# A two-layer encoder on one core: mean squares by f32 matmuls at both ends, and a new table of places

## The chip, the cores and the metric

The kernel runs on one core of a Trainium2 chip. The metric is the device time of one execution in microseconds (us), the median of several runs. The engines are TensorE (PE, with its weight loads as PEld), VectorE (DVE), ScalarE (ACT), GpSimd (POOL) and SyncE (SP, which here only starts transfers). Each works through its own list of instructions in order; an instruction waits until what it reads is there and what it overwrites is no longer needed.

## The reference

Two layers over 1024 tokens of width 1024, in float32. Each normalises, mixes tokens, and adds the result behind a gate; the first layer has two groups of attention heads side by side, the second an attention in a window of 128 tokens to either side with a sink. Cut to what matters here:

```python
def rms_norm(x, g):
    xf = x.astype(jnp.float32)
    y = xf * lax.rsqrt(jnp.mean(xf * xf, axis=-1, keepdims=True) + EPS)
    return (y * g.astype(jnp.float32)).astype(x.dtype)
...
    c_act = jax.nn.silu(c)
    for layer in range(DEPTH):
        mod = c_act @ ada_w[layer] + ada_b[layer]
        shift, scale, gate = jnp.split(mod, 3, axis=-1)
        h = rms_norm(x, norm_w[layer]) * (1.0 + scale[:, None, :]) + shift[:, None, :]
        ...  # y = even_mixer(h, ...) or odd_mixer(h, ...)
        x = x + gate[:, None, :] * y
    return rms_norm(x, final_norm)
```

The change concerns the mean of squares of the first norm (first half of the tokens) and of the last norm (last block), and the order of all work. The values computed stay the same.

## The kernel before

The activations lie transposed, features in the 128 partitions and tokens along the row: xT00 to xT03 hold the first 512 tokens, two chunks of 128 features each (128x1024), xT10 to xT13 the other 512. Every product of float32 matrices is made from three matmuls in a rounded format (fp32r): each operand is split in a high part (h, a cast) and a low part (l, operand minus high part), and high×high, low×high and high×low add up in PSUM.

The program in order: the input is loaded, its mean squares give r = (mean + eps)^-0.5 per token, h = x·r·scale + shift is built chunk by chunk (hT00h/l, ...), where scale and shift (mods) come from DVE's operations on blocks of the modulation weights (ada...). Products with the first layer's combined weights follow: w1x (416 columns, c1), w3x (512, c3) and w2 (256, c2), x the pair of feature chunks. Then the first group's attention (q, k; hl, V), the second group's (latent: khh, kll, Qa/Pa and Qb/Pb with VA/VB), the output projection in seven block products by sums and differences (a, b, s, t with numbers; o and og are the attention outputs, xr the residual rows), the second layer (T6, T7 and hT1x are its normalised inputs, wf its weights, p its windowed scores), its output projection, and the last norm.

A mean over features is a sum over partitions and chunks. At the start, ACT squares each chunk, DVE adds the squares chunk by chunk into two sums (sq0 and the last chunk's sq07), PE transposes them, and DVE reduces the transposed rows (ss), scales and adds eps; POOL raises to the power -0.5 (r, with mhalf as exponent), PE transposes r's columns, widened by broadcast, back to rows, and DVE multiplies x by them. The end has the same steps for the last block of 256 tokens, xr110 to xr113: rstd_rows and finish, called from layer1_after. xr112 is multiplied on POOL with a copy (rbz) made by ACT, the others on DVE.

Order and placing: nothing is issued where it is written. The class Recorder takes every operation down (so each instruction bears one line, L825, where emit calls it). run plans them against the engines with a duration for each from cost, and knows that DVE and POOL share a way into SBUF (held). placed then takes the steps named in PLACES out of the planned order and puts each directly behind the step it names; the pairs are (step, step ahead of it). banks_in hands out the eight banks of PSUM in the order that results; the result is fixed as the program. Transposes of the identity (warm, WARM = how many at three places of the start) compute nothing that is used; they keep PE at work.

## Time and profile before

| what | value |
|---|---|
| median of 3 runs | 1132.55 us (1132.31 to 1133.89) |
| profiled execution | 1132.69 us |
| its span | 1130.9 us |
| granted TensorE clock, mean | 0.99 |
| PE, DVE, ACT, POOL busy | 1097.5, 991.7, 749.0, 681.9 us |
| bytes moved by DMA | 183.71 MB, 162 GB/s in the mean |

The span is what the trace shows of the execution, and lies 1.8 us below its time. The page divides it into 40 slices of 28.3 us. A busy PE need not be at its peak: below full granted clock the same instructions take longer and still count as busy. Since all work bears line 825, it is told apart by the tiles it names: out<-in.

### The profile page before, as it was taken

To read this page: it belongs to the slowest core of one execution; us is meant where nothing else is said; L and a number is where in the kernel's file an instruction comes from. 1 tells how busy PE (TensorE), PEld (TensorE's weight loads), DVE (VectorE), ACT (ScalarE), POOL (GpSimd) and SP (SyncE) were. 2 spreads that over 40 slices of the span, in tenths; PEclk is the share of its full clock that TensorE was granted. 3 is DMA by queue.
4 is the path that set the end of the run, shared out by engine and by line. 5 is a ranking of instruction groups with operands and counts; after the bars stand their busy time and mean duration, and the time that the engine had idled before them with its cause. 6 is when DMAs were issued, how large, how long until landed. Compare 5 with 4: busy or idle time off the path is not lost.

```text
span 1130.9 us, 17581 instructions
## 1 busy us (share of the span) xinstructions
PE 1097.5 (97%) x5914; PEld 935.5 (83%) x5914; DVE 991.7 (88%) x1645; ACT 749.0 (66%) x1462; POOL 681.9 (60%) x666
## 2 busy tenths in 40 slices
PE   7999989999999999999999999999999999999996
PEld 6898977888877878888888878888888888887885
DVE  6978798898999989998999999998878777778997
ACT  4653444777776787887797832667677776766723
POOL 1136776989986644345546445757666775976523
PEclk8999999999999999999999999999999999999998
DMA  9978862574656196769878376301111211249403
GB/s 365 364 186 286 278 232 71 140 181 140 159 157 183 22 279 194 195 172 250 211 177 319 89 213 245 143 1 36 40 57 39 94 57 57 94 145 333 147 1 149
DMA packets 60026, 183.71 MB, mean 162 GB/s; under 512 B 7200, under 2 KB 9632, under 8 KB 58912
## 3 DMA queue, kind: packets, MB, share of 16 engines
q1 hardware_dynamic: 54464, 159.00, 40.8%
q0 software_dynamic: 4608, 22.02, 10.7%
q10 hardware_dynamic: 864, 1.57, 0.4%
q8 instruction: 46, 0.75, 0.3%
q14 instruction: 44, 0.36, 0.1%
HBM read 147.31 MB, written 70.91 MB: 193 GB/s over the span
## 4 chain that ended last, share of the span: by engine, by line
PE 81%; DVE 11%; DMA 4%; issue 2%; ACT 1%; SPq 0%; POOL 0%; POOLq 0%; DVEq 0%; ACTq 0%
PE psum L825 81%; DMA ada<-in_ada_t 2%; DVE nm L825 1%; DVE hla L825 1%; DMA w31s<-in_w_c 1%; DVE xr L825 1%; DMA w33s<-in_w_c 1%; DVE hf L825 1%; DMA relt<-in_tabs_d 1%; DVE t40l L825 0%; DVE w2l L825 0%; DVE psum L825 0%; DVE krt L825 0%; DVE s31l L825 0%; DVE T7l L825 0%
## 5 line engine op out<-in xcount | busy, mean ns | idle before, releaser
L825 DVE TENSOR_REDUCE nm<-psum 128x1 f32<-128x1024 f32 x128 | 155.5, 1218 | 16.1 <-PE psum L825 13.9
L825 POOL TENSOR_SCALAR Pb<-Pb,rs 128x1024 f32<-128x1024 f32 x64 | 75.3, 1187 | 64.6 <-DVE rs L825 57.7
L825 POOL TENSOR_SCALAR p<-p,dn 128x384 f32<-128x384 f32 (+1 forms) x128 | 70.5, 571 | 36.2 <-DVE dn L825 36.1
L825 POOL TENSOR_SCALAR Pa<-Pa,rs 128x1024 f32<-128x1024 f32 x64 | 76.4, 1222 | 25.5 <-DVE rs L825 20.9
L825 ACT ACTIVATE Pa<-psum,nm 128x1024 f32<-128x1024 f32 x64 | 71.8, 1122 | 27.7 <-DVE nm L825 18.5
L825 DVE TENSOR_TENSOR hla<-psum,hla 128x512 fp32r<-128x512 f32 x128 | 82.8, 682 | 4.8 <-ACT hla L825 4.2
L825 DVE CUSTOM_DVE_ANT_0 p<-psum,relt,sinkn 128x384 f32<-128x384 f32 (+1 forms) x128 | 70.6, 578 | 17.2 <-PE psum L825 16.5
L825 DVE TENSOR_TENSOR hlb<-psum,hlb 128x512 fp32r<-128x512 f32 x128 | 81.9, 680 | 3.2 <-ACT hlb L825 2.9
L825 PE MATMUL psum<-hla,VA 128*128 128x512 f32 x256 | 81.6, 410 | 2.9 <-DVE hla L825 2.8
L825 ACT ACTIVATE Pb<-psum,nm 128x1024 f32<-128x1024 f32 x64 | 71.9, 1124 | 17.1 <-DVE nm L825 12.2
L825 ACT ACTIVATE p<-p,nm 128x385 f32<-128x385 f32 (+1 forms) x128 | 74.8, 591 | 9.4 <-POOL p L825 4.9
L825 ACT CAST hla<-psum 128x512 fp32r<-128x512 f32 x128 | 70.0, 597 | 15.7 <-PE psum L825 13.6
L825 PE MATMUL psum<-k,q 128*128 128x512 f32 x256 | 80.3, 396 | 0.1
L825 PE MATMUL psum<-hlb,VB 128*128 128x512 f32 x256 | 79.6, 411 | 0.1
L825 PE MATMUL psum<-ident,Pa 128*128 128x128 f32 x512 | 74.5, 275 | 2.3 <-DVE cqT L825 2.2
L825 PEld LDWEIGHTS psum<-ident,Pa 128*128 128x128 f32 x512 | 62.0, 142 | 13.4 <-issue 2.8
L825 ACT CAST hlb<-psum 128x512 fp32r<-128x512 f32 x128 | 68.8, 605 | 4.4 <-PE psum L825 3.6
L825 ACT COPY ot<-psum 64x512 f32<-64x512 f32 x64 | 37.4, 584 | 50.1 <-PE psum L825 49.3
L825 ACT CAST hl<-psum 128x512 fp32r<-128x512 f32 x88 | 48.4, 590 | 33.0 <-PE psum L825 26.1
L825 DVE TENSOR_TENSOR hl<-psum,hl 128x512 fp32r<-128x512 f32 x88 | 57.7, 685 | 13.7 <-ACT hl L825 12.7
L825 PE MATMUL psum<-ident,Pb 128*128 128x128 f32 x512 | 69.0, 272 | 0.0
L825 PEld LDWEIGHTS psum<-ident,Pb 128*128 128x128 f32 x512 | 60.2, 141 | 8.0 <-ACT Pb L825 0.4
(1146 smaller groups left out, 3721.9 us busy)
## 6 DMA issues: line engine op xcount, KB each, us to landing
ada<-in_ada_t SPq DMA_DIRECT2D x32, 512.0 KB, 9.7
fs<-in_w_f POOLq DMA_DIRECT2D x12, 768.0 KB, 9.1
adag<-in_ada_t SPq DMA_DIRECT2D x16, 512.0 KB, 5.1
ws<-in_w_out POOLq DMA_DIRECT2D x16, 512.0 KB, 6.8
S<-ws SPq DMA_DIRECT2D x16, 512.0 KB, 5.3
A<-in_w_out SPq DMA_DIRECT2D x12, 512.0 KB, 6.7
o<-spill SPq DMA_DIRECT2D x12, 512.0 KB, 6.0
fs<-in_w_f SPq DMA_DIRECT2D x6, 768.0 KB, 8.5
```

Source lines behind the costliest of these rows:

```text
L825: fn(*[real(v) for v in a], **{k: real(v) for k, v in kw.items()})
```

## The change

Seven things change.

1. PLACES is another table, found by a search that the code doesn't contain; and a string BANKS gives each PSUM tile the bank to start from. cost gives a matmul that is not fp32r at least 222 ns.
2. The mean squares at the start: PE sums over partitions itself. share is a column of 128 values 1/1024; a matmul with a 128x128 block of squares as the weights and share as the moving operand adds the means of 128 tokens in one column of PSUM. 28 such f32 matmuls (8 for sq00, 8 for sq01, 4 for sq02, whose two chunks POOL adds first, 8 for sq03) replace six additions on DVE, eight transposes and two reductions. The second half of xT02's and xT03's squares moves from ACT to DVE; xT00 and xT01 are squared in one instruction each.
3. The tail: the last block's sum and the last square go through four such matmuls, with no reduction.
4. WARM goes from 32, 14, 8 to 18, 8, 6, tied by dependences: 18 ahead of the cb transposes, 8 behind the last mean-square matmul and ahead of r's transposes, 6 behind those and ahead of the first products. 54 identity transposes become 32.
5. The first chunk's multiplication by r and the high part of h are made in two halves of 256 tokens.
6. SP's first six transfers are the same in both (xT00, cols, xT01, xT02, xT03, ada000); of those behind, w10s goes ahead of w33s and w11s goes up by four places.
7. Elsewhere steps move by a few places on each engine, all with the same work.

PE at the start, before, with the products of the first chunk below (w10h, w10l: weights; ident alone: warming):

```order
L825 MATMUL psum_72<-ident_73 128x128 x31
L825 MATMUL psum_72<-ident_73,cs_82 128x128 x4
L825 MATMUL psum_72<-ident_73 128x128
L825 MATMUL psum_72<-ident_73,cs_82 128x128 x4
L825 MATMUL psum_72<-ident_73 128x128 x2
L825 MATMUL psum_72<-ident_73,sq07_130 128x128 x4
L825 MATMUL psum_72<-ident_73,sq0_124 128x128 x4
L825 MATMUL psum_72<-ident_73 128x128 x4
L825 MATMUL psum_72<-ident_73,r_133 128x128 x4
L825 MATMUL psum_72<-ident_73 128x128 x12
L825 MATMUL psum_72<-w10h0_137,hT00h0_89 128x416
```

and in the change:

```order
L899 MATMUL psum_72<-ident_73 128x128 x18
L899 MATMUL psum_72<-ident_73,cs_84 128x128 x8
L899 MATMUL psum_72<-share_80,sq00_126 128x1 x8
L899 MATMUL psum_72<-share_80,sq01_127 128x1 x8
L899 MATMUL psum_72<-share_80,sq02_128 128x1 x4
L899 MATMUL psum_72<-share_80,sq03_129 128x1 x8
L899 MATMUL psum_72<-ident_73 128x128 x8
L899 MATMUL psum_72<-ident_73,r_131 128x128 x4
L899 MATMUL psum_72<-ident_73 128x128 x6
L899 MATMUL psum_72<-w10h0_135,hT00h0_91 128x416
```

The transposes of sq07 and sq0 have become matmuls with share, in four groups that follow the four transfers; no warming transpose stands among the products any more.

On DVE at the start, w10l now stands ahead of ss, ada001 between ss and the multiplications of xT00, and w30l and ada011 between those and hT00l; before, ss came ahead of ada001, and w10l and w30l behind the multiplication of xT00.

DVE in the second group's attention, where block 5's hla are made (hla, low parts; nm, row maxima; krt, the rotated shared key), before:

```order
L825 TENSOR_TENSOR hla504_675<-psum_72,hla504_675 128x512
L825 TENSOR_TENSOR hla505_676<-psum_72,hla505_676 128x512
L825 TENSOR_TENSOR krt_723<-krt_723 128x256
L825 TENSOR_TENSOR hla506_677<-psum_72,hla506_677 128x512
L825 TENSOR_TENSOR hla507_678<-psum_72,hla507_678 128x512
L825 TENSOR_REDUCE nm_705<-psum_72 128x1
L825 TENSOR_TENSOR og('0', 2)_633<-psum_72,ot50_695 64x512
```

and in the change:

```order
L899 TENSOR_TENSOR hla504_673<-psum_72,hla504_673 128x512
L899 TENSOR_TENSOR hla505_674<-psum_72,hla505_674 128x512
L899 TENSOR_TENSOR hla506_675<-psum_72,hla506_675 128x512
L899 TENSOR_TENSOR hla507_676<-psum_72,hla507_676 128x512
L899 TENSOR_REDUCE nm_703<-psum_72 128x1
L899 TENSOR_TENSOR krt_721<-krt_721 128x256
L899 TENSOR_TENSOR og('0', 2)_631<-psum_72,ot50_693 64x512
```

The last krt has gone from between hla505 and hla506 to behind nm.

DVE in the first layer's output projection (xr, the residual's rows; psum<-psum,sa, sums of block products; t40l, a low part for a later product), before:

```order
L825 TENSOR_TENSOR psum_72<-psum_72,sa00_1342 128x512
L825 SCALAR_TENSOR_TENSOR xr010_1322<-psum_72,ngcol_88,xr010_1322 128x512
L825 TENSOR_TENSOR t40l1_1389<-o003_1345,t40h1_1388 128x512
L825 TENSOR_TENSOR psum_72<-psum_72,sa00_1342 128x512
L825 SCALAR_TENSOR_TENSOR xr010_1322<-psum_72,ngcol_88,xr010_1322 128x512
```

and in the change:

```order
L899 TENSOR_TENSOR psum_72<-psum_72,sa00_1340 128x512
L899 SCALAR_TENSOR_TENSOR xr010_1320<-psum_72,ngcol_90,xr010_1320 128x512
L899 TENSOR_TENSOR psum_72<-psum_72,sa00_1340 128x512
L899 SCALAR_TENSOR_TENSOR xr010_1320<-psum_72,ngcol_90,xr010_1320 128x512
L899 TENSOR_TENSOR t40l1_1387<-o003_1343,t40h1_1386 128x512
L899 TENSOR_TENSOR t40l1_1387<-og('0', 7)_1254,t40h1_1386 128x512
```

t40l, which stood between the first and the second pair of psum and xr010, now stands behind both.

The diff, with the table cut to its first lines:

```diff
@@ -52,7 +52,7 @@
 K2_POOL = 1
 MOD_WAY = (("dve",), ("psum",))
 E_START = (4, 4)
-WARM = (32, 14, 8)
+WARM = (18, 8, 6)
 SQ_ENG = ("dve", "pool", "pool")
 OLO_POOL = (((0, 0), (1, 0), (2, 0)), ((0, 0), (1, 0), (2, 0)))
 C2_EARLY = 4
@@ -78,265 +78,337 @@
...
-    (48, -1), (324, 105), (110, 324), (2, 1), (78, 17), (79, 78), (80, 79), (81, 80), (82, 81), (83, 82), (84, 83),
...
+    (34, -1), (99, 93), (314, 99), (31, 33), (102, 22), (136, 102), (38, 136), (171, 38), (25, 51), (30, 25),
...
+BANKS = (
...
 )
@@ -512,7 +584,7 @@
             lhs = [r for r in regs if r[0] is kw.get("lhsT")][0]
             c = n / 2.4 + 12.5
             if "float32r" not in str(lhs[6].dtype):
-                c = 4 * n / 2.4 + 12.5
+                c = max(4 * n / 2.4 + 12.5, 222)
             return c, 0
         if eng == "SP":
@@ -783,6 +855,8 @@
     def banks_in(self, seq):

         left, seen, before = {}, set(), dict(self.bank_of)
+        if BANKS:
+            before = {x: int(b) for x, b in zip(self.banks, "".join(BANKS))}
         for o in self.ops:
             for x in o.tiles:
@@ -862,6 +936,8 @@
     make_identity(tc.nc, ident)
     mhalf = const.tile([P, 16], F32, name="mhalf")
     tc.nc.vector.memset(mhalf, -0.5)
+    share = const.tile([P, 1], F32, name="share")
+    tc.nc.vector.memset(share, 1.0 / D)
@@ -953,6 +1029,16 @@
     nc.sync.dma_start(out=cols, in_=cols_d)
     mods = const.tile([P, 32], F32, name="mods")

+
+    def warm(n, behind_):
+        pt = PT(f"warm{n}")
+        for _ in range(n):
+            t_ = nc.tensor.transpose(out=pt[:, 0:P], in_=ident, identity=ident)
+            t_.deps.update(o.i for o in behind_)
+            behind_ = [t_]
+        return behind_
+
+    warmed = warm(WARM[0], [])

     cs = SM("cs")
     nc.scalar.activation(cs[:, 0:8], cols[:, C_C:C_C + 8], AF.Tanh, scale=0.5)
@@ -962,8 +1048,9 @@
     for j in range(2):
         pt = PT(f"cb{j}")
         for k in range(4):
-            nc.tensor.transpose(out=pt[:, k * P:(k + 1) * P], identity=ident,
-                                in_=cs[:, 8 + 4 * j + k:9 + 4 * j + k].broadcast_to([P, P]))
+            t_ = nc.tensor.transpose(out=pt[:, k * P:(k + 1) * P], identity=ident,
+                                     in_=cs[:, 8 + 4 * j + k:9 + 4 * j + k].broadcast_to([P, P]))
+            t_.deps.update(o.i for o in warmed)
         nc.vector.tensor_copy(cb[:, j * 512:(j + 1) * 512], pt)
     nwh = const.tile([P, 16], F32, name="nwh")
     nc.gpsimd.tensor_scalar(nwh, cols[:, C_NW:C_NW + 16], 0.5, 0.0, op0=ALU.mult, op1=ALU.add)
@@ -976,17 +1063,6 @@
     ngcol = const.tile([P, 16], F32, name="ngcol")


-    def warm(n, mark):
-        pt = PT(f"warm{mark.i}")
-        with rec.at(shift=5000), issue_after(mark):
-            for _ in range(n):
...
@@ -1022,6 +1098,45 @@
         t = U(name)[:, 0:src.shape[1]]
         nc.scalar.activation(t, src, AF.Square)
         eng.tensor_tensor(out=acc, in0=acc, in1=t, op=ALU.add)
+
+    def mean_squares(name, nt):
+
+        pt = PA(f"st{name}")
+        done = []
+
+        def add(sq, last=False):
+            for j in range(nt):
+                m_ = mm(pt[:, j:j + 1], lhsT=sq[:, j * P:(j + 1) * P], rhs=share, start=not done, stop=last,
+                        skip_group_check=True)
+                if done:
+                    m_.deps.update([x.i for x in done] if last else [done[0].i])
+                done.append(m_)
+            return m_
+
+        return pt, add
+
+    def rstd_of_means(pt, nt, name, twice=False, around=None):
+
+        ss = SM("ss")
+        nc.vector.tensor_scalar(ss[:, 0:nt], pt[:, 0:nt], 1.0, EPS, op0=ALU.mult, op1=ALU.add)
+        return broadcast_rstd(ss[:, 0:nt], nt, name, twice, around)
+
+    def broadcast_rstd(v, nt, name, twice, around=None):
+
+        n = nt * P
+        r = SM("r")
+        marks["rstd", name] = nc.gpsimd.tensor_tensor(out=r[:, 0:nt], in0=v, in1=mhalf[:, 0:nt], op=ALU.pow)
+        prs = [PA(f"rb{name}{k}") for k in range(2 if twice else 1)]
+        around = warm(WARM[1], around) if around else []
+        got = []
+        for pr in prs:
+            for j in range(nt):
+                t_ = nc.tensor.transpose(out=pr[:, j * P:(j + 1) * P], in_=r[:, j:j + 1].broadcast_to([P, P]), identity=ident)
+                t_.deps.update(o.i for o in around)
+                got.append(t_)
+        if around:
+            marks["warm"] = warm(WARM[2], got)
+        return [pr[:, 0:n] for pr in prs] if twice else pr[:, 0:n]
@@ -1041,18 +1156,7 @@
                 nc.vector.scalar_tensor_tensor(out=ss[:, 4:4 + nt], in0=ss[:, 0:nt], scalar=1.0 / D, in1=v, op0=ALU.mult,
                                                op1=ALU.add)
             v = ss[:, 4:4 + nt]
-        if name == "x0" and WARM[1]:
-            warm(WARM[1], m_)
-        r = SM("r")
-        marks["rstd", name] = nc.gpsimd.tensor_tensor(out=r[:, 0:nt], in0=v, in1=mhalf[:, 0:nt], op=ALU.pow)
-        prs = [PA(f"rb{name}{k}") for k in range(2 if twice else 1)]
-        for pr in prs:
-            for j in range(nt):
-                m_ = nc.tensor.transpose(out=pr[:, j * P:(j + 1) * P], in_=r[:, j:j + 1].broadcast_to([P, P]),
-                                         identity=ident)
-        if name == "x0" and WARM[2]:
-            warm(WARM[2], m_)
-        return [pr[:, 0:n] for pr in prs] if twice else pr[:, 0:n]
+        return broadcast_rstd(v, nt, name, twice)
@@ -1063,7 +1167,9 @@

         h, lo = hl
         if way == "normed":
-            nc.scalar.activation(h, src, AF.Identity, bias=sh_col(l, kc), scale=A_col(l, kc))
+            for o in (0, 256) if kc == 0 else (0,):
+                e = o + 256 if kc == 0 else 512
+                nc.scalar.activation(h[:, o:e], src[:, o:e], AF.Identity, bias=sh_col(l, kc), scale=A_col(l, kc))
             nc.scalar.activation(src, src, AF.Identity, bias=sh_col(l, kc), scale=A_col(l, kc))
             sub(lo, src, f(h))
@@ -1127,18 +1233,26 @@

     def xT_half(half):
         xT[half] = [U(f"xT{half}{k2}") for k2 in range(4)]
-        acc = U(f"sq{half}")
         if half == 0:
             for k2 in range(4):
                 load(xT[0][k2], xt[0, k2])
-            a, b = acc[:, 0:512], acc[:, 512:1024]
-            for kc in range(KC - 1):
-                add_squares((a, b)[kc % 2], chunk(xT[0], kc), kc < 2, f"sq0{kc}", nc.vector)
-            nc.vector.tensor_tensor(out=a, in0=a, in1=b, op=ALU.add)
-            last = U("sq07")[:, 0:512]
-            add_squares(last, chunk(xT[0], KC - 1), True, "", None)
-            return rstd_rows([a, last], "x0")
+            pt, add = mean_squares("x0", 4)
+            for k2 in range(4):
+                q = U(f"sq0{k2}")
+                a, b = q[:, 0:512], q[:, 512:1024]
+                if k2 < 2:
+                    nc.scalar.activation(q, xT[0][k2], AF.Square)
+                else:
+                    nc.scalar.activation(a, xT[0][k2][:, 0:512], AF.Square)
+                    y = xT[0][k2][:, 512:1024]
+                    nc.vector.tensor_tensor(out=b, in0=y, in1=y, op=ALU.mult)
+                if k2 == 2:
+                    nc.gpsimd.tensor_tensor(out=a, in0=a, in1=b, op=ALU.add)
+                for t in (a,) if k2 == 2 else (a, b):
+                    m_ = add(t, k2 == 3 and t is b)
+            return rstd_of_means(pt, 4, "x0", around=[m_])
         else:
+            acc = U(f"sq{half}")
             eng = nc.vector if SQ_ENG[0] == "dve" else nc.gpsimd
@@ -1162,6 +1276,8 @@
             c1[i] = PA(f"c1_{i}")
         for kc in kcs:
             m_ = mm3(c1[i][:, :416], hslice(hT0, kc, i), w[kc - kcs[0]], kc == 0, kc == KC - 1)
+            if kc == 0 and i < 4:
+                m_.deps.update(o.i for o in marks["warm"])
             if kc == kcs[0]:
                 marks["c1", i, kc // 4] = m_
@@ -1242,7 +1360,9 @@
     for kc in range(KC):
         ada_mods(0, kc, late=marks["rstd", "x0"])
         c = chunk(xT[0], kc)
-        nc.vector.tensor_tensor(out=c, in0=c, in1=rb0 if kc else rp0, op=ALU.mult)
+        for o in (0, 256) if kc == 0 else (0,):
+            y, z = (c[:, o:o + 256], rp0[:, o:o + 256]) if kc == 0 else (c, rb0)
+            nc.vector.tensor_tensor(out=y, in0=y, in1=z, op=ALU.mult)
         if kc % 2 == 0:
             w1 += wload([w_c1[kc // 2]], 416, f"w1{kc // 2}", hi_eng=START_ENG[0], lo_eng=START_ENG[1])
@@ -1989,8 +2109,13 @@
                         out=acc, in0=acc, in1=t, op=ALU.add)
             if last or half == 1 and pos < 4:
                 nc.scalar.activation(y, y, AF.Copy, scale=fn(ft))
+            if last and pos > 5:
+                if pos == 6:
+                    accs["means"] = mean_squares("zl", 2)
+                accs["means"][1](acc if pos == 6 else t, pos == 7)
             if pos == 7:
-                finish(res, half, c0, n, rstd_rows(sums, f"z{half}{c0}", last), last)
+                finish(res, half, c0, n, rstd_of_means(accs["means"][0], 2, "zl", True) if last else
+                       rstd_rows(sums, f"z{half}{c0}", last), last)
         return after
```

More of the change, by code (lines that the diff above doesn't have):

```diff
@@ L80 @@
 PLACES = (
[259 rows of a table removed]
[320 rows of a table added]
+)
+BANKS = (
+    "0232511627345101206260125476352143102732341504104052666030223154145666667777012310404243521022454040",
+    "7723230160404067106142534242107006767236242444505032526264326057320620532234670146060345554267201606",
+    "0224465746606025467016706042307635475312406040513230325027011401646467401647565613317417024640226745",
+    "3016460223670134460455342324006064073110564250626254726076420627456423560620724010561302462517574714",
+    "2660450537220200716174542424101567232462001234512624623570311426124646663451237402426736457302402637",
+    "3670104043326701454604526470162012343014423523251012320235232515167046320105342674552653657717624621",
+    "7323327331241320426751450715261206412612451625126457561432704230234540255723001231253351421423621452",
+    "6171124546675472704534700112007472126172402167574251212344724205771607205121044204476104676237210612",
+    "34316025402301054701012365354737034201370112401227016270342701333210621001",
 )
@@ L976, in encoder_kernel @@
     ngcol = const.tile([P, 16], F32, name="ngcol")
-    def warm(n, mark):
-        pt = PT(f"warm{mark.i}")
-        with rec.at(shift=5000), issue_after(mark):
-            for _ in range(n):
-                nc.tensor.transpose(out=pt[:, 0:P], in_=ident, identity=ident)
-    if WARM[0]:
-        warm(WARM[0], rec.ops[-2])
     def ada_sum(o, src, scale, first, name, mark, late=None):
@@ L1185, in c3_part @@
             m_ = mm3(c3[i], hslice(hT0, kc, i), w[kc - kcs[0]], kc == 0, kc == KC - 1)
+            if kc == 0 and i < 4:
+                m_.deps.update(o.i for o in marks["warm"])
             if kc == 0:
```

577 rows, old and new, of the table PLACES are left out of this document.

## The prediction

> **What bounds the kernel now.** I read the page first, then PE's waits, then stretches of the span, then single stretches of the timeline. The page:
>
> ```profile
> span 1130.9 us, 17581 instructions
> PE 1097.5 (97%) x5914; PEld 935.5 (83%) x5914; DVE 991.7 (88%) x1645; ACT 749.0 (66%) x1462; POOL 681.9 (60%) x666
> PE   7999989999999999999999999999999999999996
> PEclk8999999999999999999999999999999999999998
> ```
>
> TensorE is busy 97% of the span, and the change leaves its products as they are (5914 PE instructions become 5912). So nothing can be won but idle time of PE, time at a lower granted clock, and the two ends, where the first and last slices show 7 and 6 tenths. 1130.9 − 1097.5 = 33.4 us of idle PE is the ceiling without the clock. Who ends PE's waits (us in all, times, longest):
>
> ```profile
> PE psum L825 <- POOL r L825: 5.0, 2, 2.9
> PE psum L825 <- DVE xr L825: 3.6, 3, 2.4
> PE psum L825 <- DVE hla L825: 3.0, 2, 2.8
> PE psum L825 <- ACT sq L825: 2.8, 1, 2.8
> PE psum L825 <- DVE cqT L825: 2.2, 1, 2.2
> ```
>
> r is the reciprocal root of the mean squares, at the start (2.9) and at the end (2.1); sq its squares at the start; the rest are places in the middle where VectorE is late. By stretches (length, busy time of each engine, granted clock, DMA share, GB/s):
>
> ```profile
> 10.00:20.60 10.60, 5.95 (x28) 5.31 (x29) 8.44 (x15) 4.15 (x7) 2.01 (x1) 0.60 1.03 415
> 28.00:56.00 28.00, 28.00 (x136) 25.01 (x135) 28.00 (x40) 18.55 (x23) 4.05 (x3) 1.00 0.93 371
> 140.00:170.00 30.00, 26.71 (x122) 21.58 (x121) 28.75 (x26) 14.76 (x22) 23.69 (x13) 1.00 0.64 219
> 330.00:345.00 15.00, 12.21 (x60) 9.92 (x60) 13.43 (x18) 8.27 (x16) 9.36 (x9) 0.89 0.82 210
> 660.00:676.00 16.00, 13.59 (x54) 10.84 (x53) 15.28 (x15) 3.06 (x3) 8.53 (x3) 0.89 0.50 167
> ```
>
> A wait of nearly 3 us costs twice: round 335 and 668 the granted clock falls too. 0.11 × 15 = 1.65 us and 0.11 × 16 = 1.76 us of full-speed work are lost there on top of the wait. From 28 to 56 both PE and DVE are full, and DMA nearly.
>
> **The change part by part.** *The start.* The rows that set the first product:
>
> ```profile
> 7.34 1.29 DVE L825 COPY cb<-psum 128x512 f32<-128x512 f32 x2 [2.12 <-PE psum L825]
> 13.22 0.89 ACT L825 CAST w10h<-w10s 128x832 fp32r<-128x832 f32 x1 [2.45 <-DMA w10s<-in_w_c]
> 15.05 1.28 DVE L825 CUSTOM_DVE_ANT_0 ada<-ada,cb,cols 128x1024 f32<-128x1024 f32 x1
> 15.21 2.01 POOL L825 TENSOR_TENSOR r<-ss,mhalf 128x4 f32<-128x4 f32 x1 [10.09 <-DVE ss L825]
> 15.78 1.04 ACT L825 CAST w30h<-w30s 128x1024 fp32r<-128x1024 f32 x1 [1.67 <-DMA w30s<-in_w_c]
> 17.27 1.12 PE L825 MATMUL psum<-ident,r 128*128 128x128 f32 x4 [2.89 <-POOL r L825]
> 17.97 2.58 PEld L825 LDWEIGHTS psum<-ident 128*128 128x128 f32 x12
> 18.43 0.69 DVE L825 TENSOR_TENSOR xT<-xT,psum 128x512 f32<-128x512 f32 x1 [2.10 <-PE psum L825]
> 19.03 1.02 DVE L825 TENSOR_TENSOR w10l<-w10s,w10h 128x832 fp32r<-128x832 f32 x1
> 19.15 0.81 ACT L825 ACTIVATE hT00h<-xT,mods 128x512 fp32r<-128x512 f32 x1 [2.33 <-DVE xT L825]
> 20.60 0.69 PE L825 MATMUL psum<-w10h,hT00h 128*128 128x416 f32 x1
> ```
>
> Chain: squares, transposes, two reductions, r, transposes, multiply, hT00h, product. Twelve warming transposes stand in front of the product, 2.58/12 = 0.215 us each, and hold it until 20.55 though hT00h is there at 19.96.
>
> "First tokens ahead of weights" changes nothing: SP's first six transfers are the same in both kernels. What moves is w10s, ahead of w33s. The casts of w10s and w30s wait for their transfers 15.78 − 13.22 = 2.56 us apart with one transfer between, so 1.28 us a place: w10s lands at about 11.94. Cast 0.89, low part 1.02 (now ahead of the sum's finish in DVE's order), then the one small operation that replaces two reductions and two small ones: 11.94 + 0.89 + 1.02 + 0.16 (the smallest DVE step I allow, an estimate) = 14.0 instead of about 15.2. The power takes 2.01 beside a DVE operation that starts at 15.05 and 0.70 for half the columns in the tail (row below); I take 1.4, so r at 15.4 (between 14.7 and 16.0), where it was at 17.2. From r to the product took 20.60 − 17.27 = 3.3 us. Now: transposes to multiply 1.16, half a multiply 0.35, half an activation 0.41, some 0.3 of hand-over, 2.2 in all; the six warming transposes (1.3) fit beside the multiply and the activation. First product 17.6, and with 0.6 for what DVE and ACT have in between (the 1.28 operation may stand just ahead of the multiply) 18.2: **−2.4** (−3.0 to −1.2 by the two ends of r).
>
> This holds if the 28 new f32 products with one column are through by 14.0. The trace has none. Bounds by rows: a weight load of an f32 transpose, 0.105 at full clock (half the 0.215), is the least; three of the cold ones, 0.65, since this kernel makes an f32 product from three others, the most. They can start behind the cb transposes, the first four of which release the copies at 7.34, so from about 7.5 on, and a square arrives with each token transfer. 28 × 0.105 = 2.9 and 28 × 0.215 = 6.0 end at 13.5 or before; I take 0.215, the nearest row, and 0. From 0.23 each on they are late. The Trainium skill ("FP8 and Floating Point Precision", TensorE Precision Notes) says that true FP32 takes four passes through the array; an estimate by it is 0.42 each, which would put their end at 19.3. It speaks against this edit, and no row here tests it.
>
> What hides behind the start: DVE has been idle 2.10 us before the multiply, and w10l's 1.02 moves into idle time ahead of it, so DVE, as full as PE up to 56, is early by as much as PE. The transfers are not: were one of them just in time, part of the gain would stop there. I cost that at 0.4 and put the start at −2.0.
>
> *The middle.* No arithmetic changes; the table moves steps by a few places. Where PE waits longest, VectorE ran something long just ahead of what PE needed:
>
> ```profile
> 334.49 3.73 DVE L825 TENSOR_TENSOR krt<-krt 128x256 f32<-128x256 f32 x1
> 334.81 1.11 POOL L825 TENSOR_SCALAR wuqh<-wuqs 128x768 fp32r<-128x768 f32 x1
> 335.62 1.52 POOL L825 TENSOR_TENSOR og('0', 2)_633<-og('0', 2)_633,gT 64x512 f32<-64x512 f32 x1
> 336.87 1.07 POOL L825 TENSOR_SCALAR wuqh<-wuqs 128x768 fp32r<-128x768 f32 x1
> 338.88 1.12 PE L825 MATMUL psum<-hla,VA 128*128 128x512 f32 x3 [2.79 <-DVE hla L825]
> 667.04 2.87 DVE L825 TENSOR_TENSOR t40l<-o,t40h 128x512 fp32r<-128x512 f32 x1
> 666.97 2.39 POOL L825 TENSOR_TENSOR sq<-sq,sq 128x1024 f32<-128x1024 f32 x1 [2.45 <-ACT sq L825]
> 671.36 0.79 PE L825 MATMUL psum<-t30h,s30h 128*128 128x512 f32 x1 [2.41 <-DVE xr L825]
> 753.53 3.43 DVE L825 TENSOR_TENSOR T7l<-xr,T7h 128x1024 fp32r<-128x1024 f32 x1
> 756.88 1.21 DVE L825 TENSOR_TENSOR T6l<-xr,T6h 128x1024 fp32r<-128x1024 f32 x1
> 758.15 0.50 PE L825 MATMUL psum<-T6l,wf3h 128*128 128x512 f32 x1 [1.61 <-DVE T6l L825]
> ```
>
> krt on 128x256 runs 3.73 us while POOL is at work without a gap (334.81 to 337.94), where T6l on four times the elements takes 1.21 with POOL at rest. These DVE operations with two operands in SBUF stop while POOL runs. The new order takes each of the three out of the way: krt goes behind hla506, hla507 and nm; t40l behind two pairs of psum and xr; the second T6l directly behind the first, ahead of T7l. Removed in full: 2.79 + 1.65 at 335, 2.41 + 1.76 at 668, 1.61 at 756, together 10.2. What is late next: krt is still there, and POOL is busy 9.36 of 15 us round it, so nm and og may now wait, which PE needs later; t40l now stands ahead of two other pairs; T7l is needed some products later. The waits for cqT and its like at 140 to 170, with DVE at 28.75 of 30, are too much work, which an order does not take away: 0.
>
> Against it stand all other places of a new table, thousands of steps, each of which may put such a DVE operation beside POOL ahead of something PE needs. Bounds: nothing, and two such stalls at the 4.4 of the one at 335, 8.8. I take a little over one, +5.0: with POOL busy 60% of the span and DVE 88%, a step that moves meets POOL work as often as not, but few stand where PE waits within 3 us. The middle: −10.2 + 5.0 = **−5.2**.
>
> *The tail.*
>
> ```profile
> 1121.84 0.41 DVE L825 TENSOR_REDUCE ss<-psum 128x2 f32<-128x256 f32 x1
> 1122.56 0.20 DVE L825 SCALAR_TENSOR_TENSOR ss<-ss 128x2 f32<-128x2 f32 x1
> 1122.85 0.70 POOL L825 TENSOR_TENSOR r<-ss,mhalf 128x2 f32<-128x2 f32 x1
> 1125.67 1.26 POOL L825 TENSOR_TENSOR xr<-xr,rbz 128x512 f32<-128x512 f32 x1 [0.90 <-ACT rbz L825]
> ```
>
> Four f32 products of a column take the place of four transposes, the reduction of 0.41 goes, and the small step (0.20) no longer waits behind a multiply: r some 0.75 earlier, if the products cost what the transposes did; at 0.65 each (+0.9 for the last two) nothing is won. POOL's last multiply waits 0.90 for ACT's copy, which stands behind a transfer that waits for POOL itself; now it stands ahead. DVE's multiplies end only 0.75 earlier, though, and SP's last two transfers change places, so one of them waits for the later: I take **−1.1** (−1.6 to 0).
>
> Sum against the profiled execution, 1132.69 (span 1130.9 and 1.8 around it; the median of the runs is 1132.55, 0.14 lower): −2.0 − 5.2 − 1.1 = −8.3, so **1124.4 us**.
>
> **The rivals.** *The waits only move* (0.25). krt, t40l and T7l meet POOL again a few places later, and PE waits there. POOL's 60% and DVE's 88% speak for it; against it, that krt's and t40l's results are needed later than what they held up. Start 2.0 and tail 1.1 remain, and perhaps the 0.5 of half a stall: 1132.69 − 3.6 = 1129.1.
>
> *New collisions* (0.10, slower). One mechanism: a two-operand DVE step next to POOL work ahead of a matmul that waits, with 2.79 + 1.65 = 4.4 us each. The order gains 13.3 before any of them (2.0 + 10.2 + 1.1), so three (13.2) eat it up and four make 1132.69 − 13.3 + 17.6 = 1137.0. For it: every place in the table may be new. Against: before has two with a fall of the clock in 1131 us. The Trainium skill ("SBUF — State Buffer", Who interferes with whom) has an exclusive lock here, and whoever starts first keeps it for one instruction. t40l agrees: it began 0.07 behind POOL's 2.39 and took 2.87. krt does not: it began 0.32 ahead of POOL's first and sat through three.
>
> *Dear column products* (0.08). At 0.42 each, four of the warm loads, 7.5 + 11.8 = 19.3 instead of 14.0; all of the start's 2.0 and another 3.3 are lost, the tail wins half: 1124.4 + 5.3 + 0.5 = 1130.2. It decides from 0.23 us on, and above some 0.7 the kernel would be slower.
>
> **How the numbers follow.** The forecast holds 0.57, with a range of its own of 1120 to 1128; two such stalls instead of a little over one make 1128.2, none 1119.4. The rivals reach to 1129.1, 1130.2 and 1137. For 8 in 10 I take 1118.5 to 1131.0, which leaves out the collisions and some of either edge. A measurement of this kernel tells a change from none from about 0.2%, 2.3 us: faster is below 1130.3. Forecast 0.56, moved waits 0.19, dear products 0.05 and a tenth of the collisions (two or fewer) 0.02 make faster 0.82; same 0.09; slower 0.09.
>
> **What would show it.** Right: first real product (w10h, hT00h) at 17.6 to 18.8; no PE wait behind hla at 335 nor behind xr at 668, and a granted clock of 1.00 there; T6l without wait; the r of the tail followed by the end in less than 7.4 us, some 1 us less than now. The column products at about 0.2 us each. Wrong: another PE wait over 2 us with a DVE operation stretched to 3 us beside POOL; the sum's small step later than 14.5; PE waiting near 40 to 60 for a transfer, which would take the start's gain back.

## The result and the profile after

The changed kernel takes 1125.3 us (median of five runs, 1123.71 to 1128.79) against 1132.55 before: ratio 0.9939, 95% interval 0.9919 to 0.9960, so 4.5 to 9.2 us faster. 1124.4 was forecast. The profiled execution, 1123.71, is the fastest of the five; its span is 9.0 us shorter than the one of before.

The page of the changed kernel:

```profile
span 1121.9 us, 17620 instructions
PE 1097.7 (98%) x5944; PEld 938.1 (84%) x5944; DVE 975.5 (87%) x1637; ACT 747.3 (67%) x1459; POOL 682.6 (61%) x667
PEclk8999999999999999999999999999999999999999
```

PE is busy for as long as before; what went is idle time. There are 32 more PE instructions than the order lists, one for each of the 32 f32 products: each runs as two. Who ends PE's waits now (us in all, times, longest):

```profile
PE psum L899 <- ACT Pb L899: 3.3, 3, 2.0
PE psum L899 <- DMA q<-qnp: 2.6, 1, 2.6
PE psum L899 <- DVE hT00l L899: 1.8, 1, 1.8
PE psum L899 <- POOL r L899: 1.6, 2, 1.1
PE psum L899 <- DVE xr L899: 1.3, 2, 1.0
PE psum L899 <- ACT Pa L899: 1.3, 1, 1.3
PE psum L899 <- DVE T6l L899: 0.8, 1, 0.8
```

hla (3.0), sq (2.8), cqT (2.2) and most of xr and r are gone from the list; Pb (the exponentials of a block's attention) and a transfer of q, which were not on it with anything near 2 us, head it. The stretches that answer to those of before (the same work comes earlier), and two new ones:

```profile
10.00:20.60 10.60, 9.42 (x49) 8.73 (x50) 7.06 (x11) 4.02 (x6) 2.01 (x1) 0.68 1.03 413
138.00:168.00 30.00, 29.83 (x138) 24.47 (x136) 27.71 (x28) 16.05 (x24) 19.55 (x10) 1.00 0.65 213
326.00:341.00 15.00, 13.27 (x76) 10.69 (x74) 14.85 (x20) 9.75 (x19) 10.05 (x9) 1.00 0.63 164
650.00:666.00 16.00, 16.00 (x73) 13.23 (x72) 12.98 (x15) 4.74 (x5) 7.83 (x4) 1.00 0.80 280
408.00:418.00 10.00, 7.96 (x30) 6.06 (x29) 7.81 (x11) 5.05 (x9) 3.97 (x4) 0.83 0.62 250
458.00:469.00 11.00, 8.43 (x37) 6.70 (x36) 6.96 (x11) 5.08 (x9) 0.00 (x0) 0.84 0.75 193
```

The stretch round t40l is full (16.00 of 16), the one at 138 nearly (29.83 of 30, where 26.71 was), the one round krt better by 1.06. At 408 and 458 there are two holes with a fall of the clock.

To see where the time went, each product of the one trace was matched with the same product of the other (own arithmetic). So many us earlier (median of each stretch) TensorE reaches the same product, by the time in the kernel before:

```
 20-60   2.5     160-180  4.7     340-360  10.1    460-480  5.8     660-680  4.0
 60-80   1.4     180-220  5.9     400-420  12.8    500-520  4.0     680-700  7.6
120-140  1.9     320-340  7.0     420-440   9.2    560-580  3.0    1080-1100 9.1
```

So the gain is built up to 12.8 by 410, nearly ten of it are lost again at 410, 460 and up to 580, and five and a half come back behind 660, four of them at t40l. (The last product itself comes 8.4 earlier.)

### The profile page after: what moved, and what is told of

Read it like the earlier page. It is cut to its first block, busy times and chain, and to the rows that moved or that the text cites. A ratio compares the mean times of both kernels' runs of the same rounds, so it can differ in the third digit from the quotient of the medians.

```text
span 1121.9 us, 17620 instructions
## 1 busy us (share of the span) xinstructions
PE 1097.7 (98%) x5944; PEld 938.1 (84%) x5944; DVE 975.5 (87%) x1637; ACT 747.3 (67%) x1459; POOL 682.6 (61%) x667
## 4 chain that ended last, share of the span: by engine, by line
PE 82%; DVE 11%; issue 2%; ACT 2%; DMA 2%; POOL 1%; SPq 0%; POOLq 0%; ACTq 0%; DVEq 0%
PE psum L899 82%; DVE ada L899 2%; DVE xr L899 1%; DVE nm L899 1%; DMA ada<-in_ada_t 1%; DVE sq L899 1%; ACT Pb L899 1%; DMA q<-qnp 1%; DMA xT<-in_xt 1%; DVE hT00l L899 0%; DVE hf L899 0%; DVE xT L899 0%; DVE hT11l L899 0%; DVE psum L899 0%; DVE s21l L899 0%
## 5 line engine op out<-in xcount | busy, mean ns | idle before, releaser
L899 DVE TENSOR_REDUCE nm<-psum 128x1 f32<-128x1024 f32 x128 | 155.4, 1218 | 15.2 <-PE psum L899 13.5
L899 ACT ACTIVATE Pb<-psum,nm 128x1024 f32<-128x1024 f32 x64 | 71.7, 1122 | 28.6 <-DVE nm L899 18.8
L899 PEld LDWEIGHTS psum<-ident,Pa 128*128 128x128 f32 x512 | 60.8, 140 | 11.6 <-ACT Pa L899 2.1
```

The source lines that it names most:

```text
L899: fn(*[real(v) for v in a], **{k: real(v) for k, v in kw.items()})
```

## The experiments

In all of these kernels a second list, MOVES, is applied behind PLACES by the same function; each pair moves a step to directly behind another.

**1. krt alone, on the kernel before.**

```diff
+MOVES = ((2958, 2900),)          # krt behind nm
         seq = self.placed([... by planned start ...], PLACES)
+        seq = self.placed(seq, MOVES)
```

> The kernel before with one step moved on VectorE: the last krt goes from between hla505 and hla506 to behind hla507 and the row maxima nm that follow; nothing else. Theory (a two-operand VectorE step stretched by GpSimd's work stood ahead of what TensorE waits for): the wait of 2.79 us behind hla near 336 is gone, and with it the stretch at half clock that starts at 339.8; TensorE is some 4 us earlier from 345 on, and the end 3 to 4.4 us earlier, if nothing behind takes it back. Rival (the wait only moves): krt is stretched as long, nm and og are late instead, TensorE waits 2 us or more within the next 10 us, and the end moves by less than 1 us.

Measured: 1129.59 against 1131.46, ratio 0.9977 (0.9967 to 0.9987), so 1.5 to 3.7 us; in the profiled execution TensorE is 4.4 us earlier from 340 on and 3.8 at the end. VectorE's row for krt, and the stretch, of this kernel:

```profile
337.02 0.98 DVE L828 TENSOR_TENSOR krt<-krt 128x256 f32<-128x256 f32 x1
330.00:345.00 15.00, 14.68 (x85) 12.01 (x84) 14.45 (x22) 10.98 (x22) 11.38 (x10) 1.00 0.81 208
```

krt takes 0.98 instead of 3.73, PE is busy 14.68 of 15 instead of 12.21. Even the 0.98 is in part a wait: krt starts while GpSimd casts wuqh (336.64 to 337.73) and ends 0.27 behind it, as it ended 0.28 behind GpSimd's last step in the kernel before; with GpSimd idle it takes 0.42 (experiment 10). The mechanism is shown; the median falls short of the profile's 4, for a reason that the next run suggests.

**2. cqT alone, on the kernel before.** MOVES = ((1075, 1274),): the second half of cqT1 (the queries' latent, normalised and transposed) ahead of hf10, hf11 and G7l, three steps for the first layer's gate (gT and gk are others).

> The kernel before with one step moved on VectorE: the second half of cqT1 goes ahead of hf10, hf11 and G7l, behind which it stood. Theory (the waits near 147 to 178 were an order too, a stretched G7l ahead of cqT): the wait for cqT (2.2 us) falls below 0.5 and TensorE is about 2 us earlier from 150 on; the waits behind gT and gk stay, and may take some of it. Rival (too much work on VectorE between 140 and 180, as the prediction had it): the wait for cqT is replaced by longer waits behind gT and gk, and at 185 TensorE is less than 0.5 us earlier.

Measured: 1129.81, ratio 0.9989 (0.9977 to 1.0000): by the medians hardly told from no gain. In the profile the wait for cqT is gone and TensorE is 1.0 us earlier from 140 to 330: between the two expectations, as new waits behind Pa (0.41) and gk (0.23) and a longer one behind gT (1.25 for 1.13) take a good part of the 2.16. So part of the change's 4.0 there was an order, and the rest needs other moves. And without any edit there, this kernel is 1.6 us better at 335 and 1.4 at 668. Its wait behind hla and that stretch:

```profile
337.91 1.10 PE L828 MATMUL psum<-hla,VA 128*128 128x512 f32 x3 [2.79 <-DVE hla L828]
329.00:344.00 15.00, 12.21 (x70) 9.90 (x69) 14.66 (x21) 8.36 (x16) 9.35 (x9) 1.00 0.85 218
```

It is the same wait of 2.79 us as before, with a granted clock of 1.00 where it was 0.89. A wait of that length brings the clock down in one execution and not in another.

**3. Four steps, on the kernel before.** MOVES = ((2958, 2900), (5846, 5731), (6358, 6356), (1075, 1274)): krt, t40l, T7l, cqT.

> The kernel before with four steps moved on VectorE and no other change: krt behind nm, cqT ahead of G7l, t40l behind the second pair of psum and xr010, T7l behind the second T6l. If each place was worth what its wait and its fall of the clock cost, the sum is 4.4 + 2 + 4.1 + 1.6 = 12 us, less what waits anew: 1121 to 1125. Rival (the gains of the change come from the two ends and from everywhere in the table): less than 5 us, 1128 or more.

Measured: 1124.18 (1123.63 to 1124.74), ratio 0.9938 (0.9920 to 0.9955), as expected by the first theory, and as fast as the whole change. Four steps on one engine are worth what the mean squares, the warming and the new table bring together. Matched products: 1.1 at 140, 4.2 at 335, 4.1 at 668, 0.5 at 756.

**4. The changed kernel again**, beside the next three.

> The changed kernel as it is, beside the next three on the same chip: 1125.3 us as measured, its TensorE waits at 410 (2.0 us, behind Pb) and 460 (2.6 us, behind a transfer), each with a fall of the clock.

Measured: 1126.54 (1125.61 to 1129.71). The waits are there (2.68 behind Pb and 3.32 behind the transfer), but only the second brings the clock down. The start is another than in the first profile; there and here, PE's products with share, and the first real product:

```profile
6.00 3.63 PE L899 MATMUL psum<-share,sq 128*128 128x1 f32 x32
9.95 4.28 PE L899 MATMUL psum<-share,sq 128*128 128x1 f32 x24 [0.32 <-POOL sq L899]
12.27 1.03 DVE L899 TENSOR_TENSOR w10l<-w10s,w10h 128x832 fp32r<-128x832 f32 x1 [0.47 <-ACT w10h L899]
14.27 0.16 DVE L899 TENSOR_SCALAR ss<-psum 128x4 f32<-128x4 f32 x1 [0.97 <-PE psum L899]
14.51 2.01 POOL L899 TENSOR_TENSOR r<-ss,mhalf 128x4 f32<-128x4 f32 x1 [4.61 <-DVE ss L899]
19.16 0.46 PE L899 MATMUL psum<-w10h,hT00h 128*128 128x416 f32 x1 [0.65 <-ACT hT00h L899]
```

```profile
6.12 10.16 PE L899 MATMUL psum<-share,sq 128*128 128x1 f32 x56
21.21 0.71 PE L899 MATMUL psum<-w10h,hT00h 128*128 128x416 f32 x1 [0.20 <-ACT hT00h L899]
10.00:20.60 10.60, 10.07 (x48) 9.67 (x48) 5.76 (x11) 2.38 (x4) 2.65 (x2) 0.50 1.03 413
20.60:28.00 7.40, 7.20 (x26) 6.02 (x26) 7.39 (x12) 5.51 (x8) 0.00 (x0) 0.69 1.03 411
```

At full clock 16 products (32 instructions) take 3.63 us, 0.227 each; the other 12, most of them at half clock, 0.357 each. In the second execution the clock has fallen at 8.1 already and stays at half until 25.2 (from the trace's clock records; 11.1 and 17.9 in the first): the 28 products take 10.16 us (nine at 0.227 until 8.1 and, worked out from that, 19 at 0.43), and the first real product comes at 21.21, later than the 20.60 of the kernel before. TensorE had no gap from 6.12 to 16.28, and nothing but products with share, so the clock is not held by them. In all six profiled executions with one-column products (here and in the first, in experiments 5 to 7 and in 9) the clock falls between 8.1 and 11.1, for 6.8 to 17.1 us, and the first real product comes at 19.04 to 21.21.

**5. ada100 behind two row maxima, on the changed kernel.** MOVES = ((3611, 3601),). The rows that stand behind the wait at 410:

```profile
408.61 1.35 DVE L899 CUSTOM_DVE_ANT_0 ada<-ada,cb,a 128x1024 f32<-128x1024 f32 x1 [2.47 <-DMA ada<-in_ada_t]
409.88 1.22 DVE L899 TENSOR_REDUCE nm<-psum 128x1 f32<-128x1024 f32 x1
411.19 1.11 ACT L899 ACTIVATE Pb<-psum,nm 128x1024 f32<-128x1024 f32 x1 [2.88 <-DVE rs L899]
412.45 0.73 PE L899 MATMUL psum<-k,q 128*128 128x512 f32 x2 [2.04 <-ACT Pb L899]
```

VectorE waits for a modulation block's transfer; nm, Pb and PE wait behind it, one after the other.

> The changed kernel with one VectorE step moved: the modulation step ada100, which waits 2.47 us for its transfer near 406, goes from ahead of two row maxima nm to behind them. Theory (the wait behind Pb at 410 is that transfer's, handed on by VectorE's order): the wait of 2.0 us and the half clock from 413.9 are gone, and the kernel is 3 to 3.7 us faster than the change. Rival (VectorE is late there for all its work): Pb's wait shrinks by less than half, and the kernel is within 1 us of the change.

Measured: 1121.15 (1118.26 to 1123.80), ratio to the kernel before 0.9904 (0.9880 to 0.9927), where the change beside it has 0.9953 (0.9938 to 0.9967): 5.4 us between the medians, of which products matched against the execution of experiment 4 show 1.6 at 410 (there the clock did not fall at 410; against the first profile, where it did, 2.3). The rest of the difference from the execution of experiment 4 lies ahead of 20 us (2.8, another fall of the clock at the start) and at 460 (1.2). So the wait is ada100's, and worth its 1.6 and a fall of the clock at times; the median overstates it.

**6. Three loads behind the copies of k and q, on the changed kernel.** MOVES = ((4004, 3886), (4426, 3873), (4430, 4426)). The rows of SyncE's queue ahead of the wait at 460:

```profile
454.44 0.54 SPq L899 DMA_DIRECT2D ada<-in_ada_t  x1
455.58 0.54 SPq L899 DMA_DIRECT2D ada<-in_ada_t  x1
456.17 0.49 SPq L899 DMA_DIRECT2D k<-knp  x1
463.59 0.47 PE L899 MATMUL psum<-k,q 128*128 128x512 f32 x1 [2.57 <-DMA q<-qnp]
```

The profile names a copy of q as releaser. By the landing times it is the copy of k issued at 456.17, behind two loads of 512 KB, which lands at 463.45.

> The changed kernel with three issues moved in SyncE's queue: the modulation loads ada131, ada140 and ada150 (512 KB each) go from among the copies of k and q to behind them. Theory (k22, issued behind two such loads, landed at 463.45 instead of some 2.5 us earlier): the wait of 2.6 us at 460 falls below 0.5, the fall of the clock at 465 goes, and the kernel is 3 to 4 us faster than the change. Rival (qnp's own production on VectorE is late, or the copies share the transfer engines with loads that are already on the way): the wait stays above 1.5 us.

Measured: 1121.91 (1119.42 to 1123.63), ratio 0.9909 (0.9888 to 0.9931). The same stretch of this kernel:

```profile
458.00:470.00 12.00, 12.00 (x73) 10.34 (x72) 11.94 (x20) 9.49 (x18) 0.00 (x0) 1.00 0.94 237
```

PE is full, and by the matched products 5.0 us are gained at 460 (from 2.8 behind the execution of experiment 4 to 2.3 ahead). The theory holds; this execution lost 3.6 of it earlier, between 330 and 380, in a wait behind hla (1.38) and a fall of the clock (from 338.0) that the change's profiles don't have. What brought those about was not tried.

**7. Four column products less, on the changed kernel.**

```diff
-            for o in (self.ops[i] for i in seq):
+            for o in (self.ops[i] for i in seq if i not in self.skip):
...
+                if o.i in self.extra:
+                    a, b = self.extra[o.i]
+                    self.tc.nc.vector.tensor_tensor(out=b, in0=a, in1=b, op=ALU.add)
```

skip holds the four products of xT03's first chunk; extra puts the addition behind VectorE's square of the second.

> The changed kernel with the two chunks of xT03's squares added on VectorE first, so that four column products less are needed (24 instead of 28). Theory (the column products at half clock, 0.36 us each, end at 14.2 and hold ss behind w10l's 13.3; ss then meets ada001 and the power takes 2.0 instead of 1.0): ss at about 13.5, r from about 14.7 instead of 16.5, first product at 17.2 to 17.6 instead of 19.16, 1.5 to 2 us faster than the change at the start. Rival (the start hangs on the transfers: ada001's landing at 13.9 and its step, which hT00h needs too): ss earlier, the first product not, less than 0.5 us.

Measured: 1124.76, ratio 0.9939 (0.9921 to 0.9958); the intervals of this and of the change overlap. ss came at 14.14, not 13.5: w10l was through at 13.71 and TensorE later still, as the clock fell at 9.3 in the profiled execution. r took 2.00 again, and the first product came at 19.04, not 17.2 to 17.6. The theory's step failed here, the gain isn't shown: fewer products didn't help where the clock fell earlier.

**8. The mean-square products 64 columns wide, on the changed kernel.**

```diff
-                m_ = mm(pt[:, j:j + 1], lhsT=sq[:, j * P:(j + 1) * P], rhs=share, start=not done, stop=last,
+                m_ = mm(pt[:, 64 * j:64 * j + 64], lhsT=sq[:, j * P:(j + 1) * P], rhs=share.broadcast_to([P, 64]), start=not done, stop=last,
-        nc.vector.tensor_scalar(ss[:, 0:nt], pt[:, 0:nt], 1.0, EPS, op0=ALU.mult, op1=ALU.add)
+        nc.vector.tensor_scalar(ss[:, 0:nt], pt[:, 0:64 * nt:64], 1.0, EPS, op0=ALU.mult, op1=ALU.add)
```

> The changed kernel with each mean-square matmul 64 columns wide: share is repeated 64 times as the moving operand, and one column of the 64 is read. Same number of instructions, same order. Theory (one-column products keep TensorE's instruction stream full but do not hold its granted clock: it fell at 11.1 us in one execution of the change and at 8.1 us in another, and the first product came at 19.2 and at 21.2): with 64 columns the clock stays full until the wait for r at least, the last mean-square product ends at 13 to 13.5 instead of 14.2 or later, and the first product comes at 19.0 or before; the median is 1 to 2.5 us below the change's 1125.3 to 1126.5, and the spread of the runs narrows from 4 to 5 us to about 2. Rival (the clock goes by TensorE's gaps, not by columns, or by where its window falls): the fall comes as before, the first product at 19 to 21, the time is the change's.

Measured: 1122.14 (1120.01 to 1123.93), ratio 0.9911 (0.9893 to 0.9928). Its start:

```profile
6.91 6.36 PE L899 MATMUL psum<-share,sq 128*128 128x64 f32 x56
13.31 0.16 DVE L899 TENSOR_SCALAR ss<-psum 128x4 f32<-128x4 f32 x1
13.55 1.03 POOL L899 TENSOR_TENSOR r<-ss,mhalf 128x4 f32<-128x4 f32 x1 [3.56 <-DVE ss L899]
14.00 1.28 DVE L899 CUSTOM_DVE_ANT_0 ada<-ada,cb,cols 128x1024 f32<-128x1024 f32 x1 [0.53 <-DMA ada<-in_ada_t]
16.88 0.46 PE L899 MATMUL psum<-w10h,hT00h 128*128 128x416 f32 x1 [0.94 <-ACT hT00h L899]
10.00:20.60 10.60, 9.17 (x66) 8.32 (x66) 9.04 (x15) 5.00 (x7) 1.03 (x1) 1.00 1.03 414
```

Sixty-four times the columns at no cost: 28 products in 6.36 us, 0.227 each. The clock stays at 1.00 from 6.8 until the wait at 410. ss no longer waits for PE, r comes ahead of the modulation step and takes 1.03 instead of 2.01, and the first product stands at 16.88. The median lies 3.2 to 4.4 below the change's, more than the 1 to 2.5 expected. In this execution, then, the wide products hold the clock, where the one-column products of experiment 9, run beside it, lose it at 8.2. But experiment 10's kernel, with wide products too, has a fall from 12.5 to 15.9, behind two gaps in its products (rows there). So the width is shown to help in two executions against six; that it holds the clock in each, and how it is counted, isn't shown. The spread of the runs, 3.9 us, did not narrow as expected; the falls at 410 and 460 are still there.

**9. The edits of 5, 6 and 7 together.**

> The changed kernel with the three edits measured one by one: ada100 behind two row maxima, three modulation loads behind the copies of k and q, the squares of xT03 added on VectorE. Against the change beside them (1126.5) they gave 5.4, 4.6 and 1.8 us. Theory (three separate waits): they add up but for the falls of the clock counted in each, 1126.5 - 8 to - 11, so 1115.5 to 1118.5. Rival (each cure uncovers the next wait, as 410 and 460 share one cause, the modulation loads): 1119 to 1121, no better than the best of them by more than 2.

Measured: 1117.82 (1117.11 to 1118.27), ratio 0.9875 (0.9858 to 0.9892): 8.7 us below experiment 4's median, of 11.8 if all were added, so within the range of the first theory, which took off the falls counted in each. Both falls of the clock in the middle are gone, and so is the spread.

**10. These, the wide products, and two steps more.** MOVES gets (2948, 3079), krt behind wuql1, and (4768, 5011), ada171 behind two row maxima.

> As the one before, with three edits more: krt moved on to behind wuql1, where GpSimd is idle; ada171, stretched to 2.65 us ahead of nm at 556, behind two row maxima; the mean-square matmuls 64 columns wide. Theory: the waits of 0.6 and 1.5 us at 333 to 336 behind og and Pa and of 1.0 at 560 behind Pb go, and the start gains 1 to 2: 1111 to 1115. Rival (waits below 2 us without a fall of the clock are made up elsewhere): within 1.5 us of the kernel with three edits.

Measured: 1113.32 (1112.11 to 1116.14), ratio 0.9840 (0.9820 to 0.9859): 18 us below the kernel before, some 12 below the change. The first theory holds: at 340 to 380 the matched products gain another 1.8. Its products at the start, the stretch, and krt with GpSimd idle:

```profile
6.34 3.68 PE L902 MATMUL psum<-share,sq 128*128 128x64 f32 x32
10.53 1.10 PE L902 MATMUL psum<-share,sq 128*128 128x64 f32 x8 [0.50 <-POOL sq L902]
10.00:20.60 10.60, 8.76 (x49) 7.68 (x49) 9.61 (x17) 5.24 (x8) 1.51 (x2) 0.84 1.03 412
339.85 0.42 DVE L902 TENSOR_TENSOR krt<-krt 128x256 f32<-128x256 f32 x1
```

The gaps of 0.50 at 10.0 and 0.25 at 11.6 stand ahead of the fall at 12.5; whether they bring it about was not tried. The first product comes at 17.70, 0.8 later than in experiment 8.

## Why the prediction was right, point by point

The time lay 0.9 us above the forecast, but the parts are not those of the sum. By the profiled executions (9.0 us of span, where the medians differ by 7.25, since the profiled run is the fastest): the start to 80 us gave 1.4, the middle 7.0, the tail 0.6; forecast were 2.0, 5.2 and 1.1. In the execution of experiment 4 the start to 80 us lost 0.6 instead. Of the signs that the prediction named, those at 335 and 668 came: no wait behind hla or xr, and a clock of 1.00. The first product (19.16 and 21.21, not 17.6 to 18.8), T6l without a wait (0.8) and the tail did not.

*The start.* The step that failed is "I take 0.215, the nearest row, and 0" for the 28 column products. w10l was through at 13.30, earlier than the 13.85 of the working, and ss stood ready for it; it waited 0.97 for PE. The price at full clock, 0.227, was right to 6%, and just under the 0.23 from which they were to be late. But it was reckoned at a clock that they do not hold: at half clock they take 0.43, and in the second execution 19 of 28 ran so. The rival "dear column products" is thus true in part. The estimate of 0.42 by the Trainium skill's four passes ("FP8 and Floating Point Precision", TensorE Precision Notes) is not the price at full clock, where a product runs as two instructions in 0.227; it is near the one at half clock, and would have given a first product at 23 where the worst seen is 21.2. r was mis-sized too: 2.01 for the 1.4 taken, since ss came when ada001 did; experiment 8 shows 1.03 where r began 0.45 ahead of that step. And the bounds of the start were mis-added: r between 14.7 and 16.0, with the same 2.2 and 0.6 behind it, gives −3.1 to −1.8, not −3.0 to −1.2; the 1.44 measured lies outside. The 0.6 "for what DVE and ACT have in between" was about right (16.52 to 19.16 is 2.64 for the 2.2 + 0.6). What the prediction left at nothing came in as well: in the first execution the products from 20.6 on ran at full clock, which makes 2.5 at 20 to 60 out of 1.44 at the first product. Of that, a wait of 1.83 for hT00l at 58 took 1.1 back; before, the same wait was 0.64. It is a wait for VectorE, not for a transfer, which the prediction had feared.

*The three places.* 668 gave 4.1 of the 4.2 counted. 335 gave 3.1 of 4.4: krt met POOL again behind nm, and TensorE waited 0.4 for og and 1.3 for Pa; og and nm, from which Pa is made, the prediction had named. The rows of the changed kernel:

```profile
329.79 2.95 DVE L899 TENSOR_TENSOR krt<-krt 128x256 f32<-128x256 f32 x1
329.93 1.52 POOL L899 TENSOR_TENSOR og('0', 2)_631<-og('0', 2)_631,gT 64x512 f32<-64x512 f32 x1
331.19 1.27 POOL L899 TENSOR_SCALAR wukvh<-wukv 128x1024 fp32r<-128x1024 f32 x1
336.06 0.44 PE L899 MATMUL psum<-ident,Pa 128*128 128x128 f32 x2 [1.30 <-ACT Pa L899]
```

krt began 0.14 ahead of POOL's og and ended 0.28 behind wukvh: once more it sat through two POOL instructions that started behind it. So here too the order of starting, as the profile has it, did not decide, against the rule of the Trainium skill that the prediction weighed ("SBUF — State Buffer", Who interferes with whom). One thing is open: when krt began, POOL was issuing a transfer (329.33 to 330.12; in the kernel before, 334.22 to 335.04), and whether that held the way into SBUF for POOL was not tried. 756 gave 0.5 of 1.6: the two T6l, side by side now, were themselves stretched. "Removed in full", with the clock, was too simple a price: experiment 2 shows the wait of 2.79 without a fall, so the 1.7 us of a fall belong to some executions only, and the medians hold a part of them.

*140 to 180.* Here the prediction put 0: "too much work, which an order does not take away". Wrong: 4.0 us came from there, over a third of what the middle gained up to 400. Not all of VectorE's 28.75 of 30 busy were work: the steps that start between 140 and 170 take 30.2 us together, the same steps 27.5 in the change, and 23.4 if each took the shortest time of its form in the two traces (own arithmetic). Experiment 2 got 1.0 of it by one step.

*New waits.* +5.0 was taken; about 9.8 came between 400 and 580 (12.8 to 3.0). That is above the 8.8 of its bound, two stalls, and the mechanism was another: for most of it not VectorE beside GpSimd, but modulation loads, among the copies of k and q in SyncE's queue (in the kernel before none stands there) or not yet landed, ahead of something that TensorE waits for (experiments 5 and 6). Only ada171 at 556, stretched to 2.65, is of the kind that was described. The gain of 2.7 at 345 to 400, from waits of 0.4 to 0.8 each, was not counted either; the two misses, 6.7 gained and 4.8 lost, happen to offset.

*The tail.* 0.6 of 1.1, within its bounds. From the last product to the end it is 11.13 us before and 10.52 after. r comes 0.8 earlier against the last product, and POOL's two multiplies follow each other without ACT's copy between:

```profile
1113.65 0.69 POOL L899 TENSOR_TENSOR r<-ss,mhalf 128x2 f32<-128x2 f32 x1
1114.32 2.49 POOL L899 TENSOR_TENSOR xr<-xr,rbz 128x512 f32<-128x512 f32 x2
```

But from r's start to the end it is 8.25 us, where it was 8.05 and the prediction wanted less than 7.4. The rows of the last transfers say where the rest went: the last one is issued 0.6 earlier behind r than before, but three are issued within 0.4 us (1116.78 to 1117.16), and the last lands 3.48 us behind its issue, where before it took 2.62. That they hold each other up fits this, but was not tried.

So the size was right by terms that were wrong on both sides: a gain at 140 to 400 left out, new waits set too low, the start too hopeful. What the three places would give was understood; that the total came within 0.9 us was luck.

## What to carry to other kernels

A VectorE that is 95% busy beside GpSimd is not yet a reason to expect nothing from its order: look how long the same form takes where GpSimd rests before calling it work (krt: 0.42, where it stood at 3.73). When a table of the order changes, look for each long or late step (a stretched one, or one that waits for a transfer) at what stands right behind it on its engine; four such moves were worth as much as the whole change, and the same look at the changed kernel brought 12 us more. Where small matmuls fill TensorE's list ahead of large ones, look at the granted clock in several executions: one profile of this start showed 19.2 us, another 21.2.

## What the runs showed of the hardware

- Products with one moving column do not hold TensorE's granted clock though they follow each other without a gap: from 6.12 to 16.28 us without one, at half clock from 8.1 on; six executions of six have such a fall. With 64 columns, at the same 0.227 us each, one execution stayed at 1.00, and one fell for 3.41 us behind gaps of 0.50 and 0.25.
- An f32 product with 128x128 weights and one column runs as two instructions: 0.227 us at full clock, 0.43 at half (worked out from 19 in the rest of 10.16 us).
- The same wait of 2.79 us is followed by a fall of the clock for 3.41 us in one execution (0.89 over 15 us) and by none in another (1.00).
- POOL's power on 128x4 took 2.01 us where a VectorE step of 1.28 ran beside it, 1.03 where it came 0.45 ahead of that step.
- A VectorE step with two operands in SBUF (krt) ended 0.27 to 0.28 us behind a run of GpSimd's steps each time that it met one: 3.73 and 2.95 us where it started 0.32 and 0.14 ahead of that run, 0.98 where it started 0.38 behind the start of its last step, and 0.42 with GpSimd idle.
